# The scale, shift and gate vectors of a two-layer diffusion block: from 32-column matmuls to multiply-and-sum passes of VectorE

## The chip, the cores and the metric

The kernel runs on one core of a Trainium2 chip. The metric is the device time of one execution in microseconds: the median of three executions is 1672.93 us (1672.89 to 1675.74). About 0.2%, some 3.3 us, is what such a measurement can tell from no change.

## The reference

Two layers, each a token mixer and a mixture of experts, on 512 tokens (256 of context, 256 latent) of 1024 features. Ahead of each layer a conditioning vector gives six vectors of 1024: shift, scale and gate for the mixer and for the experts, for both conditions (context and latent).

```python
silu_c = jax.nn.silu(c)[:, None, :]
silu_cc = jax.nn.silu(c_ctx)
for l in range(DEPTH):
    sh1, sc1, g1, sh2, sc2, g2 = jnp.split(silu_c @ w_ada[l] + b_ada[l], 6, axis=-1)
    sh1c, sc1c, g1c, sh2c, sc2c, g2c = jnp.split(silu_cc @ w_ada[l] + b_ada[l], 6, axis=-1)
    hl = modulate(rmsnorm(xl, norm1[l]), sh1, sc1)
    hc = modulate(rmsnorm(xc, norm1[l]), sh1c, sc1c)
    yc, yl = token_mixer(hc, hl, ...)
    xl = xl + g1 * yl
    ...
```

`w_ada[l]` is 1024 x 6144 in float32, 24 MB a layer. The last layer needs of the context no more than shift and scale of the mixer.

## The kernel before

Features lie on the 128 partitions, tokens along the free axis. The program has four parts, one behind the other: the mixer of layer 0 (to about 640 us), the experts of layer 0 (to about 1040), the mixer of layer 1 (to about 1330) and the experts of layer 1.

**Products.** A weight matrix is used in units of two 128-row blocks, 512 KB each, which SyncE's queue loads into slots named `w` and `wa` (`Pipe.load_unit`, L161). Each unit is split into a high and a low part: ScalarE copies the high one (L102), VectorE subtracts (L103, 128x1024 elements). TensorE then makes three products for each block and chunk (`mm3`, L88 to L90) into four banks of PSUM. `Pipe` splits one unit ahead of the one in use.

**Modulation.** `ada` holds the six vectors as 48 chunks of 128 for each layer and both conditions. The first 2048 columns of layer 0 (shift and scale of the mixer, chunks 0 to 15) are made at the start from eight loads of 1 MB, in four steps that also give the normalised input `h`. All others come in half pieces of 512 columns (class `Ada`, L257): a half piece is 1 MB, loaded in two DMAs (`ada_load`, L252), and four matmuls (L283) whose stationary operand has 32 columns, of which two hold the silu of the conditions; the four write 32 rows each of one shared bank. Four pieces fill a bank; `finish` copies it (L294), sums and turns it by eight small matmuls (L297, records of both passes) and adds the bias (L304). A float32 matmul leaves two records in the profile.

**Where this work stands.** `tick` (L311) does one half piece behind each unit of weights that a product has used (`Pipe.matrix`, L204), from the gate projections of the mixer of layer 0 on. So 32 half pieces (layer 0's columns from 2048 on, layer 1's up to 4096) stand in the second half of that mixer. The last eight belong to the mixer of layer 1: five at its start (`TAIL`), while its norm is computed, and three in its first product.

**The order.** A scheduler lays out each engine's queue from the program, and may put an instruction ahead of others that stand before it in the code if its inputs and its buffer allow. Each engine then works strictly in that order. Around the change stand the norm and the first projections (`attention_proj`), the softmax tiles of the attention (`attention`: a score matmul L539, then on VectorE the maximum L541, its negative L543, after ScalarE's exponential L546 the reciprocal L548 and the scaling L549, then transposes on TensorE), the recurrence (`mlstm`), and three gated branches with two products per half (`branch`).

## Time and profile before

| | |
|---|---|
| median of three executions | 1672.93 us |
| span of the profiled execution | 1671.4 us |
| TensorE busy | 1582.0 us, 95% of the span |
| VectorE busy | 933.6 us, 56% |
| ScalarE busy | 712.6 us, 43% |
| GpSimd busy | 134.3 us, 8% |
| moved by DMA | 358.28 MB, mean 214 GB/s |

The profile gives the profiled execution's span from its first to its last instruction; the runs' own time lies around it, 1.5 us more at the median. Busy shares are averages over four parts with different limits, so what an edit is worth is read from the stretch in which it stands: in the mixer of layer 0 TensorE is busy nearly all the time and VectorE about half of it; in the experts of layer 0 both are close to full; in those of layer 1 the DMA queues are.

### The profile page before, as it was taken

What the parts mean: (1) busy time and instruction counts of PE and PEld (TensorE: products, weight loads), DVE (VectorE), ACT (ScalarE), POOL (GpSimd) and SP (SyncE); (2) the same over time, 40 slices, a digit from 0 to 9 for tenths busy, and PEclk for the clock granted to TensorE, in tenths of its full rate; (3) what the DMA queues carried; (4) which work ended last, traced back from release to release, by engine and by line L of the source; (5) the groups of instructions that cost most, each with busy time, mean ns of one, the idle gap of its engine ahead of it and who ended that gap; (6) DMA issues with size and microseconds to landing.
All of it is one profiled execution on the core that took longest, in us unless ns stands there. A gap on an engine that the chain in (4) does not pass through costs nothing. (4 is left out here: it accounts for less than half of the span.)

```text
span 1671.4 us, 22964 instructions
## 1 busy us (share of the span) xinstructions
PE 1582.0 (95%) x8611; PEld 1136.9 (68%) x8611; DVE 933.6 (56%) x1832; ACT 712.6 (43%) x1188; POOL 134.3 (8%) x128
## 2 busy tenths in 40 slices
PE   6999999999999999798989999999999998999998
PEld 3677767755567887577767776787689997453343
DVE  3565654723333443787877987567568666132223
ACT  2444336323232232476766786535466553110102
POOL 1000000000200011411211111010002001000000
PEclk8999999999999999799999999999999999999999
DMA  9222211476666375578998997623235776999996
GB/s 320 84 65 64 64 51 53 126 224 227 216 215 206 95 232 212 166 243 306 315 348 286 350 367 242 202 75 93 64 89 163 252 239 234 316 387 386 387 386 226
DMA packets 191210, 358.28 MB, mean 214 GB/s; under 512 B 13934, under 2 KB 30894, under 8 KB 190832
## 3 DMA queue, kind: packets, MB, share of 16 engines
q1 hardware_dynamic: 184160, 341.10, 60.4%
q0 software_dynamic: 6640, 15.53, 3.4%
q8 instruction: 70, 1.15, 0.3%
q14 instruction: 52, 0.43, 0.1%
q10 hardware_dynamic: 288, 0.07, 0.0%
HBM read 351.77 MB, written 12.60 MB: 218 GB/s over the span
## 5 line engine op out<-in xcount | busy, mean ns | idle before, releaser
L103 DVE TENSOR_TENSOR wlo<-wraw,whi 128x512 fp32r<-128x512 f32 (+4 forms) x356 | 322.2, 920 | 282.0 <-ACT whi L102 257.2
L102 ACT ACTIVATE whi<-wraw 128x512 fp32r<-128x512 f32 (+4 forms) x358 | 279.9, 802 | 356.0 <-PE mm L89 286.4
L88 PE MATMUL mm<-h,whi 128*128 128x512 f32 (+1 forms) x672 | 234.1, 354 | 4.1 <-ACT h L400 3.7
L89 PE MATMUL mm<-h,whi 128*128 128x512 f32 (+1 forms) x672 | 235.0, 353 | 0.0
L90 PE MATMUL mm<-h,wlo 128*128 128x512 f32 (+1 forms) x672 | 232.5, 351 | 1.3 <-DVE wlo L103 1.2
L88 PEld LDWEIGHTS mm<-h,whi 128*128 128x128 f32 x672 | 126.7, 190 | 35.8 <-issue 8.3
L89 PEld LDWEIGHTS mm<-h,whi 128*128 128x128 f32 x672 | 127.2, 190 | 30.9 <-issue 17.2
L90 PEld LDWEIGHTS mm<-h,wlo 128*128 128x128 f32 x672 | 126.9, 189 | 28.8 <-issue 12.1
L103 DVE TENSOR_TENSOR whl<-wraw,whl 128x1024 fp32r<-128x1024 f32 (+1 forms) x110 | 115.0, 1068 | 16.7 <-ACT whl L102 16.7
L1619 PE MATMUL mm<-wraw,x 128*64 128x512 f32 x504 | 121.2, 596 | 0.0
L102 ACT ACTIVATE whl<-wraw 128x1024 fp32r<-128x1024 f32 (+1 forms) x112 | 101.0, 931 | 19.9 <-issue 8.5
L283 PE MATMUL adps<-adw,sc 128*32 128x512 f32 (+1 forms) x448 | 80.3, 551 | 10.2 <-DMA adw<-in_w_ada 10.2
L1619 PEld LDWEIGHTS mm<-wraw,x 128*64 128x64 f32 x504 | 36.7, 137 | 67.5 <-issue 63.4
L88 PE MATMUL mm<-by,whi 128*128 128x512 f32 (+1 forms) x192 | 66.1, 344 | 0.0
L90 PE MATMUL mm<-whi,h 128*128 128x512 f32 x160 | 65.7, 413 | 0.0
L90 PE MATMUL mm<-by,wlo 128*128 128x512 f32 (+1 forms) x192 | 65.5, 341 | 0.0
L89 PE MATMUL mm<-by,whi 128*128 128x512 f32 (+1 forms) x192 | 65.2, 340 | 0.0
L88 PE MATMUL mm<-whi,h 128*128 128x512 f32 x160 | 65.0, 410 | 0.1
L89 PE MATMUL mm<-wlo,h 128*128 128x512 f32 x160 | 65.1, 407 | 0.0
L1570 PE MATMUL py<-wraw,gt 128*64 128x512 f32 x256 | 63.8, 598 | 0.7 <-ACT gt L1560 0.7
L88 PE MATMUL mm<-whi,x 128*128 128x512 f32 x128 | 53.6, 420 | 8.5 <-ACT whi L102 8.4
L546 ACT ACTIVATE pr<-sc,nm 128x512 f32<-128x512 f32 (+1 forms) x48 | 29.5, 615 | 62.6 <-DVE nm L543 59.6
(447 smaller groups left out, 2941.0 us busy)
## 6 DMA issues: line engine op xcount, KB each, us to landing
wraw<-in_e_w SPq DMA_DIRECT2D x278, 512.0 KB, 8.5
wraw<-in_w_in SPq DMA_DIRECT2D x96, 512.0 KB, 3.8
adw<-in_w_ada SPq DMA_DIRECT2D x80, 512.0 KB, 4.4
wraw<-in_e_w SPq DMA_DIRECT2D x33, 1024.0 KB, 13.4
wraw<-in_e_w SPq DMA_DIRECT2D x76, 256.0 KB, 6.1
adw<-in_w_ada SPq DMA_DIRECT2D x8, 1024.0 KB, 11.8
wraw<-in_w_out SPq DMA_DIRECT2D x16, 512.0 KB, 5.2
wraw<-in_w_pb SPq DMA_DIRECT2D x8, 512.0 KB, 4.8
```

The lines of the kernel that those rows point to most:

```text
L88: nc.tensor.matmul(ps, lh, rh, start=first, stop=False)
L89: nc.tensor.matmul(ps, lh, rl, start=False, stop=False)
L90: return nc.tensor.matmul(ps, ll, rh, start=False, stop=last)
L102: g.nc.scalar.activation(hi, src, AF.Copy)
L103: (eng or g.nc.vector).tensor_tensor(lo, src, hi.bitcast(F32), op=ALU.subtract)
L283: nc.tensor.matmul(self.ps[r:r + 32, :], g.sc62[:, k, 30 - 2 * j:62 - 2 * j], raw, start=(j == 0 and k < 4), stop=(j == n - 1 and k >= 4))
L546: last = nc.scalar.activation(pr[:, 0:w], sc[:, 0:w], AF.Exp, scale=ASC, bias=nm, accum_out=rs)
L1570: nc.tensor.matmul(py[hs, :], gt[:, k, hs], raws[s][:, kk, :], start=(k == 0), stop=(k == 3))
L1619: nc.tensor.matmul(ph[w][hs, :], x[:, k, hs], raws[s][:, kk, :], start=(k == 0), stop=(k == KT - 1))
```

## The change

The first four steps of layer 0 (chunks 0 to 15) stay as they were. All other chunks of both layers are no longer matmuls. The host passes their weights transposed (`w_adt`: one row of 1024 floats for each output feature). The silu of both conditions is spread once, at the start, over all partitions (`cbc`, two rows of 1024 on each partition: 16 small matmuls and four copies). For each chunk of 128 output features one load of 512 KB brings 128 rows, and VectorE makes one pass for each condition: multiply the rows by `cbc`, sum along the free axis from the bias on, write the sum into `ada`. Layer 0's chunks 16 to 47 and layer 1's 0 to 15 take two passes each, layer 1's 16 to 47 one pass (the latent condition; the other column is set to zero once): 48 chunks x 2 and 32 x 1, 128 passes in all. The transposed weights have two slots of their own (`ad`), and a step asks for the load of the next chunk. Ticks begin right behind the norm in both mixers. `w` and `wa` now alternate throughout. To make room, the descriptor space of GpSimd's own DMAs is cut to 2048 bytes a partition and `sc62` moves into a slot that is used again.

```diff
-LATER = 8
-TAIL = 5
-START1 = 8
-START0 = 18
-TAGS = dict(a=9, w=2, wa=2, wh=2, wl=2, h=8, t2=4, e1=2, e2=2, cz=2, b2=6)
+TAGS = dict(ad=2, a=9, w=2, wa=2, wh=2, wl=2, h=8, t2=4, e1=2, e2=2, cz=2, b2=6)
...
+class Rows:
+    def __init__(self, g, chunks):
+        self.g, self.chunks = g, list(chunks)
+        self.raws, self.k = [], 0
+
+    def left(self):
+        return len(self.chunks) - self.k
+
+    def load(self, n):
+        g = self.g
+        while len(self.raws) < min(n, len(self.chunks)):
+            l, j, _ = self.chunks[len(self.raws)]
+            raw = g.t([P, D], F32, "ad", "adw")
+            r = (j - 16 if l == 0 else 32 + j) * P
+            g.nc.sync.dma_start(raw, g.w_adt[r:r + P, :])
+            self.raws.append(raw)
+
+    def step(self):
+        g = self.g
+        self.load(self.k + 2)
+        l, j, conds = self.chunks[self.k]
+        raw = self.raws[self.k]
+        for s in conds:
+            out = raw if s == conds[-1] else g.t([P, D], BF16, "t2", "prod")
+            g.nc.vector.tensor_tensor_reduce(out=out, in0=raw, in1=g.cbc[:, s, :], scale=1.0,
+                                             scalar=g.vec[l][:, C_BADA + j:C_BADA + j + 1], op0=ALU.mult, op1=ALU.add,
+                                             accum_out=g.ada[l][:, j, s:s + 1])
+        self.raws[self.k] = None
+        self.k += 1
...
 def tick(g, n=1):
     for _ in range(n):
-        if g.pending:
-            b = g.pending[0]
-            b.step()
-            if not b.left():
-                g.pending.pop(0)
+        if g.rows.left():
+            g.rows.step()
...
 def mixer(g, l):
     if l == 0:
-        g.pipe = Pipe(g, lambda i: ("w", "wa")[i % 2] if i < START0 else "w", 1, ["w"])
+        g.pipe = Pipe(g, lambda i: ("w", "wa")[i % 2], 1, ["w"])
...
     else:
-        g.pipe = Pipe(g, lambda i: "w" if i < START1 else ("w", "wa")[i % 2], 1, ["w"])
+        g.pipe = Pipe(g, lambda i: ("w", "wa")[i % 2], 1, ["w"])
...
-        g.pipe.load(1)
+        g.pipe.load(2)
         g.pipe.single = True
-        b = g.pending[0]
-        raws = [b.load("h", i) for i in range(TAIL)]
-        for i in range(TAIL):
-            b.step(raws[i])
-        g.pipe.load(2)
...
-        g.ticking = True
+    g.ticking = True
     yb, gates, conv_q, last = attention_proj(g, l)
...
-    if l == 0:
-        g.ticking = True
     smo, gv, gu = gate_proj(g, l)
...
     if l:
+        tick(g, g.rows.left())
         g.router = router_prep(g, l)
...
     if l == 0:
-        tick(g, sum(b.left() for b in g.pending))
+        tick(g, g.rows.left())
...
-    g.sc62 = const("sc62", [P, KT, 62])
+    g.sc62 = g.t([P, KT, 62], F32, "b2", "sc62")
...
+    nc.gpsimd.memset(g.ada[1][:, 16:48, 0:1], 0.0)
...
-    g.pending = [Ada(g, l, range(a, b)) for l, a, b in ((0, 4, 8), (0, 8, 12), (1, 0, 4), (1, 4, LATER))]
+    g.cbc = const("cbc", [P, 2, D])
+    for s in range(2):
+        for q in range(2):
+            pc = g.bank([P, 512], "pcc")
+            for c in range(4):
+                nc.tensor.matmul(pc[:, c * P:(c + 1) * P], g.sc62[:, q * 4 + c, 30 + s:31 + s].to_broadcast([P, P]), g.ident, start=True, stop=True)
+            dst = g.cbc[:, s, q * 512:(q + 1) * 512]
+            if q:
+                nc.vector.tensor_copy(dst, pc)
+            else:
+                nc.scalar.activation(dst, pc, AF.Copy)
+    g.rows = Rows(g, [(0, j, (0, 1)) for j in range(16, 48)] + [(1, j, (0, 1)) for j in range(16)])
...
-    g.pending = [Ada(g, 1, range(LATER, 12))]
+    g.rows = Rows(g, [(1, j, (1,)) for j in range(16, 48)])
...
-    A['w_ada'] = f('w_ada')
+    A['w_ada'] = f('w_ada')[0:1, :, 0:2 * D]
+    wt = f('w_ada').transpose(0, 2, 1)
+    A['w_adt'] = np.concatenate([wt[0, 2 * D:], wt[1]], axis=0)
...
-    nc = _bacc.Bacc("TRN2", target_bir_lowering=False, num_devices=1)
+    nc = _bacc.Bacc("TRN2", target_bir_lowering=False, num_devices=1, dynamic_dma_scratch_size=2048)
```

How the change moves instructions is shown at three places. Line numbers of the changed kernel differ: its L99 is the subtraction L103 of before, its L84 to L86 are the products L88 to L90, its L333 is the new pass.

TensorE, in the gate projections and first branch of the mixer of layer 0 (`adps` is the shared bank of the modulation, `adw` its weights; each row of two is half of a half piece). Before:

```order
L88 MATMUL mm<-h,whi 128x512
L89 MATMUL mm<-h,whi 128x512
L283 MATMUL adps<-adw,sc_71 32x512 x2
L90 MATMUL mm<-h,wlo 128x512
L88 MATMUL mm<-h,whi 128x512
```

Now, at the change from the first branch product to the second (`by` is the attention's output, split):

```order
L86 MATMUL mm<-h,wlo 128x512
L84 MATMUL mm<-by,whi 128x512
L85 MATMUL mm<-by,whi 128x512
L86 MATMUL mm<-by,wlo 128x512
L84 MATMUL mm<-by,whi 128x512
```

The products stand next to each other; from the first score matmul of layer 0 on, no matmul of the modulation is left in the program.

VectorE, in the fourth softmax tile of the attention of layer 0 (`mx` maximum, `nm` its negative, `arc` reciprocal, `pr` probabilities, `pts` transposed probabilities, `va` values). Before:

```order
L541 TENSOR_REDUCE mx<-sc 128x1
L478 TENSOR_TENSOR rt<-mm,rope 128x256
L543 TENSOR_SCALAR nm<-mx 128x1
L479 TENSOR_TENSOR rt<-mm,rope 128x256
L103 TENSOR_TENSOR wlo<-wraw,whi 128x1024
L548 RECIPROCAL arc<-ars 128x1
L549 TENSOR_SCALAR pr<-pr,arc 128x256
L555 COPY pts<-pt 128x256
```

Now (each pass is a row `L333 ISA` of 128x1024 and, behind it, the read-out of its sum; a chunk's first pass writes its products to `prod`, its second over the weights):

```order
L567 TENSOR_REDUCE mx<-sc 128x1
L333 ISA prod,ada_132<-adw,cbc,vec_78 128x1024
L333 ISA ada_132 128x1
L569 TENSOR_SCALAR nm<-mx 128x1
L333 ISA prod,ada_132<-adw,cbc,vec_78 128x1024
L333 ISA ada_132 128x1
L574 RECIPROCAL arc<-ars 128x1
L333 ISA adw,ada_132<-adw,cbc,vec_78 128x1024
L333 ISA ada_132 128x1
L575 TENSOR_SCALAR pr<-pr,arc 128x256
L333 ISA adw,ada_132<-adw,cbc,vec_78 128x1024
L333 ISA ada_132 128x1
```

Passes now stand between the steps of a softmax. Of the 128 passes 28 stand ahead of the first maximum of layer 0's attention, 40 between the first and the seventeenth of its 32, 4 behind that, and 56 behind the recurrence, those of layer 1's chunks 16 to 47 among them: the scheduler has put all of these ahead, into the mixer of layer 0, and the mixer of layer 1 has none.

VectorE, at the third step of the modulation that stays (the bias is added, then `A` is the scale, `u` and `h` the normalised input). Before:

```order
L304 TENSOR_TENSOR ada_132<-adpo,vec_78 128x4 x2
L374 SCALAR_TENSOR_TENSOR A<-ada_132,vec_78 128x4
L399 SCALAR_TENSOR_TENSOR u<-xT,A,rr 128x256 x3
L401 SCALAR_TENSOR_TENSOR h<-u,ada_132,h 128x256
```

Now:

```order
L99 TENSOR_TENSOR wlo<-wraw,whi 128x1024 x2
L333 ISA prod,ada_132<-adw,cbc,vec_78 128x1024
L333 ISA ada_132 128x1
L300 TENSOR_TENSOR ada_132<-adpo,vec_78 128x4
L333 ISA adw,ada_132<-adw,cbc,vec_78 128x1024
L333 ISA ada_132 128x1
L300 TENSOR_TENSOR ada_132<-adpo,vec_78 128x4
L400 SCALAR_TENSOR_TENSOR A<-ada_132,vec_78 128x4
L425 SCALAR_TENSOR_TENSOR u<-xT,A,rr 128x256 x3
```

The first passes stand ahead of the third part of `h`.

In SyncE's queue the loads of the transposed weights now stand one or two at a time between those of the mixer of layer 0, from behind its fourth unit to its last branch; the sixteen half-megabyte loads at the start of the mixer of layer 1 are gone. On TensorE 320 products of 128x512 stand between the first and the seventeenth score matmul of layer 0, where there were 177.

## Rows read from the trace of the kernel before

**Rows 1.** The page: span, and busy time, share and instructions of two engines.

```profile
span 1671.4 us, 22964 instructions
...
PE 1582.0 (95%) x8611; PEld 1136.9 (68%) x8611; DVE 933.6 (56%) x1832; ACT 712.6 (43%) x1188; POOL 134.3 (8%) x128
```

**Rows 2.** Table by stretches of the mixer of layer 0, from start to end.

```profile
core 0: us, PE busy (x) PEld busy (x) DVE busy (x) ACT busy (x) POOL busy (x), PEclk, DMA share, GB/s
25.00:126.00 101.00, 95.76 (x512) 69.95 (x513) 56.85 (x128) 39.56 (x70) 4.05 (x2) 0.95 0.38 119
126.00:201.00 75.00, 74.37 (x390) 53.48 (x389) 46.07 (x114) 32.76 (x68) 0.00 (x0) 1.00 0.22 64
201.00:275.00 74.00, 73.81 (x385) 52.53 (x384) 35.11 (x84) 34.47 (x71) 0.00 (x0) 1.00 0.18 50
320.00:425.00 105.00, 99.81 (x413) 53.82 (x412) 33.72 (x50) 30.15 (x33) 3.14 (x4) 1.00 0.70 225
425.00:640.00 215.00, 214.01 (x985) 153.48 (x983) 82.51 (x119) 59.98 (x87) 19.82 (x28) 1.00 0.63 203
```

**Rows 3.** The same table, of the modulation's matmuls (`adps`) alone.

```profile
core 0: us, PE busy (x) PEld busy (x) ACT busy (x), PEclk, DMA share, GB/s
320.00:560.00 240.00, 59.02 (x256) 8.17 (x256) 2.40 (x4) 1.00 0.65 209
1056.00:1075.00 19.00, 3.17 (x16) 0.45 (x16) 0.60 (x1) 1.00 0.75 228
```

**Rows 4.** Timeline of TensorE around half of a half piece.

```profile
start us, us, engine line op out<-in xcount [idle before <-releaser]
341.50 0.39 PE L90 MATMUL mm<-h,wlo 128*128 128x512 f32 x1
341.73 0.39 PE L88 MATMUL mm<-h,whi 128*128 128x512 f32 x1
342.05 1.05 PE L283 MATMUL adps<-adw,sc 128*32 128x512 f32 x4
343.03 0.50 PE L89 MATMUL mm<-h,whi 128*128 128x512 f32 x1
```

**Rows 5.** Timeline of TensorE at the turning of a full bank.

```profile
371.78 0.39 PE L90 MATMUL mm<-h,wlo 128*128 128x512 f32 x1
372.01 0.95 PE L297 MATMUL adpo<-lsel,ev 128*128 128x8 f32 x8
372.82 0.48 PE L88 MATMUL mm<-h,whi 128*128 128x512 f32 x1
```

**Rows 6.** Waits for the modulation's weights, 320 to 560: total us, times, longest.

```profile
PE adps L283 <- DMA adw<-in_w_ada: 5.5, 6, 2.3
```

**Rows 7.** The same, start of the mixer of layer 1 (1053 to 1075).

```profile
PE adps L283 <- DMA adw<-in_w_ada: 0.9, 1, 0.9
```

**Rows 8.** Timeline of TensorE and VectorE at the norm of layer 1.

```profile
1045.53 2.96 PE L283 MATMUL adps<-adw,sc 128*32 128x512 f32 x20
...
1046.03 0.69 DVE L345 COPY sp<-ss 128x512 f32<-128x512 f32 x1 [1.89 <-PE ss L337]
...
1046.74 0.06 DVE L615 MEMSET mp<- 8x5 f32 x1
...
1048.42 1.05 PE L347 MATMUL sst<-lsel,sp 128*128 128x1 f32 x8
```

**Rows 9.** Groups of VectorE by shape: busy us, mean ns, idle before.

```profile
L103 DVE TENSOR_TENSOR wlo<-wraw,whi 128x1024 fp32r<-128x1024 f32 x150 | 182.8, 1221 | 210.5 <-ACT whi L102 187.2 <-PE mm L90 22.3 <-DMA wraw<-in_e_w 0.3
...
L399 DVE SCALAR_TENSOR_TENSOR u<-xT,A,rr 128x256 f32<-128x256 f32 x22 | 9.6, 476 | 1.7 <-PE rr L364 1.6
L401 DVE SCALAR_TENSOR_TENSOR h<-u,ada,h 128x256 fp32r<-128x256 f32 x22 | 9.6, 479 | 0.1
...
L849 DVE SCALAR_TENSOR_TENSOR yg<-pg,vec,gbs 128x128 f32<-128x128 f32 x24 | 6.7, 339 | 4.1 <-PE pg L845 4.1
...
L617 DVE TENSOR_TENSOR_SCAN Mr<-ar,mp 8x128 f32<-8x128 f32 x8 | 3.8, 469 | 0.1
```

**Rows 10.** Group of ScalarE: the read-out of a sum.

```profile
L546 ACT ACTIVATION_READ_ACCUMULATOR pr<-sc,nm 128x1 f32 x48 | 9.3, 194 | 0.0
```

**Rows 11.** Timeline of VectorE: first and seventeenth maximum of layer 0's attention.

```profile
127.86 0.41 DVE L541 TENSOR_REDUCE mx<-sc 128x1 f32<-128x256 f32 x1
...
200.95 0.42 DVE L541 TENSOR_REDUCE mx<-sc 128x1 f32<-128x256 f32 x1
```

**Rows 12.** Two shorter stretches, columns as in Rows 2.

```profile
100.00:125.00 25.00, 21.79 (x95) 16.98 (x93) 19.19 (x52) 11.61 (x21) 4.05 (x2) 0.86 0.22 71
300.00:325.00 25.00, 24.62 (x182) 21.05 (x182) 22.18 (x58) 11.35 (x23) 2.49 (x2) 1.00 0.41 127
```

**Rows 13.** Timeline of TensorE: two waits, at 19 and at 116 us.

```profile
19.45 1.93 PE L283 MATMUL adps<-adw,sc 128*32 128x256 f32 x16 [3.72 <-DMA adw<-in_w_ada]
...
115.97 0.96 PE L90 MATMUL mm<-nhl,wlo 128*128 128x512 f32 x3 [2.66 <-DVE wlo L103]
```

**Rows 14.** The page: loads of the modulation's weights, KB each, us to landing.

```profile
adw<-in_w_ada SPq DMA_DIRECT2D x80, 512.0 KB, 4.4
```

More of the change, by code (lines that the diff above doesn't have):

```diff
@@ L1706, in block_kernel @@
     g.nc, g.tc = nc, tc
-    g.w_ada, g.w_in, g.w_gk, g.w_uq2, g.a_wukv = w_ada, w_in, w_gk, w_uq2, a_wukv
+    g.w_ada, g.w_adt, g.w_in, g.w_gk, g.w_uq2, g.a_wukv = w_ada, w_adt, w_in, w_gk, w_uq2, a_wukv
     g.x_t = x_t
```

2 lines of the change are left out of this document (1 added, 1 removed).

## The prediction, made before the changed kernel ran

> **What bounds the kernel now.** I read the busy times of the page first: TensorE is busy for 1582 of 1671.4 us, VectorE for 934 [rows 1]. An average over four parts says little, so the table by stretches comes next, for the mixer of layer 0, where nearly all of the removed work stands. The reader should compare two columns there: TensorE is busy for 94 to 100% of every stretch, VectorE for 56.9 of 101 us ahead of the attention, 46.1 of 75 in its first half, 35.1 of 74 in its second, and for less than 40% from 320 us on [rows 2]. So TensorE bounds the mixer, and what leaves its queue there shortens the mixer by as much, if nothing else gets in its way. Where it does wait, the waits view and the timeline say for what: between 320 and 560 for the modulation's own weights [rows 6].
>
> **What is removed in the mixer of layer 0.** Its modulation matmuls fill 59.0 us of TensorE between 320 and 560 [rows 3]. That these are on TensorE's path and not beside other matmuls shows in the timeline: products follow each other every 0.23 us (341.50, 341.73), and around one group of modulation matmuls the next product starts 1.30 us behind the last, 1.07 more than the pace, which is the group's own 1.05 [rows 4]. Four banks are turned by small matmuls; there the next product starts 1.04 us behind the last, 0.81 more than the pace [rows 5], 4 x 0.81 = 3.2. And TensorE stands still for 5.5 us until these weights have landed [rows 6]. Together 59.0 + 3.2 + 5.5 = **67.7 us**.
>
> **What is removed in the mixer of layer 1.** Its first product holds 3.2 us of such matmuls [rows 3], one turning of 0.8 and one wait of 0.9 [rows 7], 4.9 in all. Ahead of it five half pieces stand beside the norm. That chain is short of work for TensorE, so most of them cost nothing; but twenty records fill TensorE from 1045.53 on, and the small norm matmul, whose input VectorE has ready at 1046.72, starts at 1048.42 [rows 8]: 1.7 us. Together 4.9 + 1.7 = **6.6 us**. The mixer of layer 1 gets no passes in return, by the order.
>
> So 67.7 + 6.6 = **74.3 us** of TensorE's path go.
>
> **What a pass costs.** The trace has no multiply-and-sum. The nearest row is the subtraction of two 128x1024 operands in SBUF, 1.22 us [rows 9]; reading out the sum is bounded by VectorE's shortest instruction, 0.06 [rows 8], and ScalarE's read-out of a sum, 0.19 [rows 10]. I take 1.22 + 0.15 = 1.37 us. From above I bound the pass by the one row in which VectorE carries a value from element to element, the scan: over 128 elements it takes 469 ns where a plain operation of this width takes 339 [rows 9], 130 ns / 128 = 1.0 ns an element more. For 1024 elements that is 1.22 + 1.04 + 0.15 = 2.4 us. I take the lower value, because a sum needs no scan and the subtraction has the same operands; the upper one is kept as a rival. 128 passes x 1.37 = 175 us of VectorE, against 74 taken from TensorE: the change pays only where VectorE was idle.
>
> **Where the passes lie.** By the order all 128 stand in the mixer of layer 0.
> - Ahead of the attention, 25 to 126 us: 28 x 1.37 = 38.4 on top of 56.9 [rows 2], 95 of 101 us.
> - First sixteen softmax tiles, 127.9 to 201.0, 73 us [rows 11]. Here 40 passes, 54.8 us, join 46.1 [rows 2]; the scheduler has also moved 320 - 177 = 143 products here, which brings 143 x 0.23 = 33 us for TensorE and six subtractions, 7 us, for VectorE. VectorE then has 108 us of work, TensorE 73 + 33 = 106.
> - Second half of the attention: 4 passes, hidden in a stretch half idle.
> - Behind the recurrence: 56 passes, 77 us, on top of 33.7 + 82.5 = 116 [rows 2], 193 in all. TensorE keeps 320 us, less 67.7, less the 33 that moved forward: 219. They fit, beside the products, which use weights split one unit ahead.
>
> So the passes are covered by TensorE's products, but in the first two stretches the cover is used up, and what is late next is a softmax step or a split on which TensorE waits. From below this costs about 1.5%: at 300 to 325 us VectorE was busy for 22.2 of 25 us and TensorE still for 24.6 [rows 12]. Over 101 + 106 us that is 3. [...] I take **17 us**, nearer to the lower row since the scheduler has put enough products between the softmax steps: 8 ahead of the attention, where the first passes stand in front of the third part of the input and wait for a load; 2 for the two us by which VectorE has more work than TensorE in the softmax tiles; 5 for sixteen softmax steps that each find a pass in front of them for 0.6 us on average, half of it covered; 2 for the clock.
>
> **What costs nothing, and why.** Spreading the silu puts 16 small matmuls and four copies of some 0.7 us (the copy of that size) [rows 8] ahead of the norm; the first modulation step waits for its weights until 19.45, 3.7 us [rows 13], and covers the two copies of VectorE in its path. SyncE's queue gets 80 loads of 512 KB, 40 MB, in the mixer of layer 0 in place of 32, and 8 MB fewer in layer 1; the queues are at 0.20 to 0.38 of their time to 275 us, where most of the moved loads go [rows 2]. A chunk of two passes, 2.7 us, needs a load that lands in 4.4 [rows 14]; with one more chunk in its second slot and 3 us of other VectorE work per chunk, it is in time, unless the queue is held up (a rival). If that cover is gone, each chunk costs up to 4.4 - 2.7 = 1.7 us.
>
> **The sum.** The page gives the span, 1671.4 us; the median of the runs, 1672.9, lies 1.5 above it, and I count that as what lies around the span. 1672.9 - 67.7 - 6.6 + 17 = 1615.6, say **1616 us**. The ends of the unknown cost give 1602 and 1655.
>
> [...] Two rows bear on operands in SBUF: the operation on `h` and `u`, both in SBUF, takes 479 ns, the one with `rr` in PSUM 476 [rows 9]; a second float32 operand in SBUF costs nothing there, but neither row keeps a sum. [...]
>
> **Rivals.**
> 1. *Slower: passes at the scan's pace.* Place: VectorE ahead of the attention and in its first half. At 2.4 us a pass VectorE has 56.9 + 67 = 124 us of work ahead of the attention where TensorE has 101, 53 + 96 = 149 in the sixteen tiles against 106, and 116 + 134 = 250 behind the recurrence, less 8 that moved, against 219: 23 + 43 + 23 = 89 us too much, and 10 more for the softmax steps. 1672.9 - 74.3 + 99 = **1698**. The loss begins where these excesses reach 74: at about 2.2 us a pass. For it: the scan's row; against it: the subtraction's and the two rows without a penalty. Chance 0.09.
> 2. *Faster, but less: passes wait for their loads.* VectorE works in order, so a pass whose rows haven't landed holds every split behind it. 34 chunks up to the seventeenth tile x 1.7 us is 58 at worst; two fifths of it on top of the forecast, 24, gives **1640**. For it: two slots only, and a queue shared with the weights; against: the free DMA time [rows 2]. Chance 0.14.
> 3. *No change.* If something other than TensorE paced the second half of the mixer, the time would stay at **1672**. Against it: 99.8 of 105 and 214 of 215 us busy, and DMA at 0.63 to 0.70 [rows 2]. Chance 0.03.
>
> **How the numbers follow.** The forecast has 0.74. The range runs from 1595, a cost of 3 us and 7 for what the sum may have missed (loads and buffers of the modulation that no longer hold up others), to 1655, the upper bound of the stall; the second rival lies in it, the first and third don't. Faster by over 0.2% (3.3 us, what a measurement can tell): 0.74 + 0.14, less 0.01 for a second rival at its worst: 0.87. Same: 0.03 and that 0.01: 0.04. Slower: 0.09.
>
> **What would show it right or wrong.** Right: no modulation matmul behind 60 us; passes of 1.2 to 1.4 us; the recurrence of layer 0 ends at about the same time as before or somewhat later (more products are behind it by then), the mixer of layer 0 some 50 us earlier, that of layer 1 about 6 us shorter; VectorE busy above 90% between 25 and 230 us and TensorE idle for about 15 us there. Wrong: passes of 2 us or more; waits of VectorE for the transposed weights of more than 20 us; TensorE waiting for VectorE in the branches behind the recurrence; or experts of layer 0 that start late because their first loads now come behind the modulation's.

## The result, and the profile after

The changed kernel takes **1634.62 us** (median of four runs, 1633.29 to 1636.02) against 1674.01 for the kernel before on the same chip: ratio 0.9759, 95% interval 0.9739 to 0.9778. It is faster by 39.4 us; the forecast was 57. The time lies in the range that was given, and the sign is right; 18 us of the expected gain are missing. The experiments look for these.

The page of the changed kernel, its span and the busy time of each engine:

```profile
span 1631.5 us, 22596 instructions
PE 1519.4 (93%) x8283; PEld 1137.8 (70%) x8283; DVE 1083.0 (66%) x2085; ACT 710.5 (44%) x1185; POOL 129.7 (8%) x129
```

Against [rows 1], TensorE has some 63 us less, VectorE 149 more. The passes and their read-out, with what VectorE waited for ahead of them (columns: ns of one, shortest/median/longest; first and last start in us):

```profile
L333 DVE DVE_READ_ACCUMULATOR2_ANT ada<- x128: 70/83/89, 47.3 to 555.6; 128x1 f32 x128
L333 DVE CUSTOM_DVE_ANT_0 adw<-adw,cbc,vec x80: 1178/1280/1291, 47.4 to 554.4; 128x1024 f32<-128x1024 f32 x80
L333 DVE CUSTOM_DVE_ANT_0 prod<-adw,cbc,vec x48: 1265/1278/2772, 46.1 to 445.2; 128x1024 bf16<-128x1024 f32 x48
...
its engine sat idle before it (us, times) until:
  DMA adw<-in_w_adt: 29.6, 27
```

A pass is 1.28 + 0.08 = 1.36 us; the forecast took 1.37. All 128 lie between 46 and 556 us, in the mixer of layer 0, as the order had it.

Three marks show where the time went: the first maximum of the attention (`mx`), the first ST of the recurrence, the first output of the mixer. In each row the first start that is named (the time behind the three durations) belongs to layer 0. Of the kernel before:

```profile
L541 DVE TENSOR_REDUCE mx<-sc x48: 411/690/692, 127.9 to 1216.6; 128x1 f32<-128x512 f32 x32, 128x1 f32<-128x256 f32 x16
L745 ACT ACTIVATE ST<-pst x6: 597/598/647, 276.3 to 1243.8; 128x512 f32<-128x512 f32 x6
L1049 DVE SCALAR_TENSOR_TENSOR xT<-mm,ada,xT x24: 472/474/485, 641.7 to 1397.3; 128x256 f32<-128x256 f32 x24
```

Of the changed kernel:

```profile
L567 DVE TENSOR_REDUCE mx<-sc x48: 414/688/692, 148.1 to 1176.4; 128x1 f32<-128x512 f32 x32, 128x1 f32<-128x256 f32 x16
L771 ACT ACTIVATE ST<-pst x6: 597/597/599, 332.6 to 1203.6; 128x512 f32<-128x512 f32 x6
L1069 DVE SCALAR_TENSOR_TENSOR xT<-mm,ada,xT x24: 474/477/485, 608.0 to 1356.1; 128x256 f32<-128x256 f32 x24
```

- **Ahead of the attention** it lost 148.1 - 127.9 = 20.2 us.
- **From there to the first ST** 184.5 us in place of 148.4, 36.1 more. By the order 158 more products stand ahead of the first `pst` (850 against 692), and at the pace of [rows 4], 0.23, they take 36.3. So the softmax tiles lost nothing. The seventeenth maximum, for [rows 11], in the timeline of VectorE, with a pass right behind it:

```profile
254.37 0.42 DVE L567 TENSOR_REDUCE mx<-sc 128x1 f32<-128x256 f32 x1
254.82 1.29 DVE L333 CUSTOM_DVE_ANT_0 prod<-adw,cbc,vec 128x1024 bf16<-128x1024 f32 x1
```

- **From the first ST to the first output** 275.4 us in place of 365.4. Without 67.7 us of modulation and the 36.3 of products that moved, it should be 261.4: 14.0 us lost. It is rather 17: behind the first output 118 products of 128x512 are left where 104 were (counted in the traces, to the last output), and 14 x 0.23 = 3.2 us of work have thus left this stretch too.

The sum, 20.2 - 0.2 + 14.0 = **34 us of stall**, stands where the prediction had 17. The mixer of layer 0 comes out 33.7 us earlier (641.7 to 608.0), which is 67.7 - 34. Its last output, with the 14 products behind it as well, comes 33.0 us earlier (667.05 to 634.09), so the stall is 34 to 35 us by either mark.

The table by stretches shows both places (columns as in [rows 2]: busy time of PE, PEld, DVE, ACT, POOL; granted clock; DMA share; GB/s):

```profile
25.00:50.00 25.00, 20.53 (x136) 13.03 (x134) 11.92 (x27) 6.55 (x12) 0.00 (x0) 0.84 0.96 310
50.00:75.00 25.00, 23.60 (x97) 19.13 (x98) 22.42 (x44) 9.78 (x19) 0.00 (x0) 0.92 0.50 169
75.00:100.00 25.00, 24.55 (x114) 16.69 (x113) 15.78 (x25) 7.65 (x13) 0.00 (x0) 1.00 0.41 141
100.00:125.00 25.00, 17.55 (x89) 14.23 (x89) 20.61 (x54) 7.13 (x12) 0.00 (x0) 0.81 0.29 92
125.00:150.00 25.00, 20.60 (x86) 16.54 (x85) 21.36 (x43) 9.52 (x19) 4.72 (x2) 0.78 0.32 106
375.00:400.00 25.00, 14.18 (x64) 10.93 (x63) 19.88 (x37) 15.78 (x17) 14.07 (x20) 0.91 0.29 88
400.00:425.00 25.00, 19.71 (x92) 15.23 (x91) 23.92 (x49) 2.12 (x2) 0.00 (x0) 0.95 0.48 165
```

TensorE, 21.79 of 25 us at 100 to 125 before [rows 12], has 17.55, and its clock falls on average to 0.81. Three things can be read from the trace as the cause, and each became a theory.

1. **The start.** ScalarE has two splits of weights ahead of the third modulation step's copy (`ev`) and waits for their loads; TensorE waits for `ev` (4.3 us, the 45.21 row below). Timelines of ScalarE and TensorE:

```profile
36.38 1.06 ACT L98 ACTIVATE whi<-wraw 128x1024 fp32r<-128x1024 f32 x1 [2.57 <-DMA wraw<-in_w_gk]
43.83 1.06 ACT L98 ACTIVATE whi<-wraw 128x1024 fp32r<-128x1024 f32 x1 [6.39 <-DMA wraw<-in_w_gk]
44.80 0.37 ACT L290 ACTIVATE ev<-adps 128x256 f32<-128x256 f32 x1
...
45.21 1.01 PE L293 MATMUL adpo<-lsel,ev 128*128 128x4 f32 x4 [4.27 <-ACT ev L290]
```

2. **The gate chain.** The recurrence's gates are some twenty small operations that go to and fro between VectorE and TensorE, from `gS` to `nM` (lines 604 to 676). Passes stand between them; in the waits of TensorE, 90 to 130, one row has nearly all (columns: us in total, times, longest):

```profile
PE mm L84 <- DVE mp L644: 6.7, 1, 6.7
```

The granted clock falls in this wait, from 1.00 at 118.5 to 0.50 from 119.5 us on. Between 121 and 128.5 TensorE is busy all the time at 0.50, and products follow each other every 0.43 us, where [rows 4] has 0.23 (rows of TensorE's timeline, then of the table by stretches):

```profile
120.68 0.77 PE L84 MATMUL mm<-nhl,whi 128*128 128x512 f32 x1 [6.73 <-DVE mp L644]
127.61 0.63 PE L84 MATMUL mm<-nhl,whi 128*128 128x512 f32 x1
128.03 0.63 PE L85 MATMUL mm<-nhl,whi 128*128 128x512 f32 x1
...
121.00:128.50 7.50, 7.50 (x24) 5.95 (x24) 5.44 (x25) 0.31 (x1) 0.00 (x0) 0.50 0.14 51
```

3. **GpSimd behind the recurrence.** The scheduler now has twelve of the router's diagonal matrices ahead of the last two squares. VectorE waits for these, ScalarE's square root for VectorE, the next split for the square root, TensorE for the split (8.6 us). One row of each engine's timeline, in the order of the chain:

```profile
376.66 8.37 POOL L1122 TENSOR_SCALAR diag<-ident,A 128x128 f32<-128x128 f32 x12 [11.96 <-DVE dn L800]
...
386.07 0.69 DVE L842 TENSOR_REDUCE ms<-sqg 128x4 f32<-128x512 f32 x1 [4.41 <-POOL sqg L841]
...
392.90 0.32 ACT L860 ACTIVATE ms<-ms,eps 128x32 f32<-128x32 f32 x1 [6.52 <-DVE ms L842]
...
399.05 0.80 PE L86 MATMUL mm<-by,wlo 128*128 128x512 f32 x1 [8.59 <-DVE wlo L99]
```

### The profile page after: what moved, and what is told of

The parts are those of the page before. It is cut to its first block, busy times and chain, and to the rows that moved or that the text cites. A ratio compares the mean times of both kernels' runs of the same rounds, so it can differ in the third digit from the quotient of the medians.

```text
span 1631.5 us, 22596 instructions
## 1 busy us (share of the span) xinstructions
PE 1519.4 (93%) x8283; PEld 1137.8 (70%) x8283; DVE 1083.0 (66%) x2085; ACT 710.5 (44%) x1185; POOL 129.7 (8%) x129
## 5 line engine op out<-in xcount | busy, mean ns | idle before, releaser
L99 DVE TENSOR_TENSOR wlo<-wraw,whi 128x512 fp32r<-128x512 f32 (+4 forms) x356 | 321.4, 917 | 130.9 <-ACT whi L98 127.6
L84 PE MATMUL mm<-h,whi 128*128 128x512 f32 (+1 forms) x672 | 236.8, 359 | 9.6 <-DVE bt L934 3.3
L85 PE MATMUL mm<-h,whi 128*128 128x512 f32 (+1 forms) x672 | 237.5, 354 | 0.0
L86 PE MATMUL mm<-h,wlo 128*128 128x512 f32 (+1 forms) x672 | 234.2, 354 | 1.3 <-DVE wlo L99 1.1
L84 PEld LDWEIGHTS mm<-h,whi 128*128 128x128 f32 x672 | 129.2, 194 | 34.6 <-DVE bt L934 6.0
L86 PEld LDWEIGHTS mm<-h,wlo 128*128 128x128 f32 x672 | 128.9, 193 | 20.4 <-issue 3.0
L85 PEld LDWEIGHTS mm<-h,whi 128*128 128x128 f32 x672 | 129.9, 193 | 18.6 <-issue 4.3
L99 DVE TENSOR_TENSOR whl<-wraw,whl 128x1024 fp32r<-128x1024 f32 (+1 forms) x110 | 115.1, 1069 | 15.2 <-ACT whl L98 15.2
L1639 PE MATMUL mm<-wraw,x 128*64 128x512 f32 x504 | 121.2, 596 | 0.0
L333 DVE CUSTOM_DVE_ANT_0 adw<-adw,cbc,vec 128x1024 f32<-128x1024 f32 x80 | 101.9, 1279 | 24.5 <-DMA adw<-in_w_adt 24.5
L86 PE MATMUL mm<-by,wlo 128*128 128x512 f32 (+1 forms) x192 | 65.4, 343 | 8.6 <-DVE wlo L99 8.6
L84 PE MATMUL mm<-by,whi 128*128 128x512 f32 (+1 forms) x192 | 66.0, 344 | 2.2 <-ACT sg L920 2.2
L333 DVE CUSTOM_DVE_ANT_0 prod<-adw,cbc,vec 128x1024 bf16<-128x1024 f32 x48 | 62.6, 1309 | 5.2 <-DMA adw<-in_w_adt 5.1
L84 PE MATMUL mm<-whi,h 128*128 128x512 f32 x160 | 65.4, 413 | 0.1
L86 PE MATMUL mm<-whi,h 128*128 128x512 f32 x160 | 64.8, 405 | 0.0
L84 PE MATMUL mm<-whi,x 128*128 128x512 f32 x128 | 53.6, 420 | 8.7 <-ACT whi L98 8.6
```

The costliest lines, as they stand in the source:

```text
L84: nc.tensor.matmul(ps, lh, rh, start=first, stop=False)
L85: nc.tensor.matmul(ps, lh, rl, start=False, stop=False)
L86: return nc.tensor.matmul(ps, ll, rh, start=False, stop=last)
L99: (eng or g.nc.vector).tensor_tensor(lo, src, hi.bitcast(F32), op=ALU.subtract)
L333: g.nc.vector.tensor_tensor_reduce(out=out, in0=raw, in1=g.cbc[:, s, :], scale=1.0, scalar=g.vec[l][:, C_BADA + j:C_BADA + j + 1], op0=ALU ...
L1639: nc.tensor.matmul(ph[w][hs, :], x[:, k, hs], raws[s][:, kk, :], start=(k == 0), stop=(k == KT - 1))
```

## The experiments

`issue_after` in the diffs queues an instruction behind a named one of the same engine. No pass is left out, except in the last two runs. All marks of the runs, from one profile of each, in us (outputs: from the start of the first output of the mixer to that of the last; experts: from there to the first output of the experts of layer 0, called their end here; mixer 1: from there to the first output of the mixer of layer 1). The order of VectorE, ScalarE and GpSimd ahead of the first maximum is the same in the changed kernel and in the run on GpSimd's order, and yet that mark differs by 2.2 us; a single difference of two microseconds therefore shows little. Each group of four runs was timed beside the kernel before, which took 1677.2, 1676.4 and 1674.7 us there; so ratios are compared.

| run | first maximum | to first ST | to first output | outputs | experts | mixer 1 | us | ratio, 95% interval |
|---|---|---|---|---|---|---|---|---|
| before | 127.9 | 148.4 | 365.4 | 25.4 | 363.7 | 354.3 | | 1 |
| changed | 148.1 | 184.5 | 275.4 | 26.1 | 361.0 | 348.8 | 1634.6 | 0.9759 (0.9739 to 0.9778) |
| GpSimd order | 145.9 | 184.0 | 273.8 | 26.1 | 363.6 | 348.3 | 1631.1 | 0.9721 (0.9703 to 0.9739) |
| start | 138.3 | 184.4 | 270.4 | 26.1 | 368.2 | 365.7 | 1639.4 | 0.9760 (0.9740 to 0.9780) |
| gates | 137.4 | 184.9 | 271.7 | 26.1 | 363.4 | 370.4 | 1643.6 | 0.9793 (0.9777 to 0.9810) |
| all three | 137.4 | 185.6 | 270.2 | 26.1 | 365.2 | 367.3 | 1638.8 | 0.9762 (0.9745 to 0.9778) |
| clean start | 137.3 | 183.6 | 276.2 | 26.1 | 363.8 | 348.8 | 1627.9 | 0.9717 (0.9683 to 0.9751) |
| late passes | 147.6 | 177.1 | 270.5 | 31.8 | 367.9 | 348.6 | 1632.3 | 0.9739 (0.9706 to 0.9772) |
| quiet chain | 124.9 | 180.8 | 272.2 | 28.7 | 365.4 | 348.8 | 1610.6 | 0.9617 (0.9583 to 0.9652) |
| quiet, late, GpSimd | 124.6 | 180.9 | 267.4 | 33.9 | 365.3 | 348.4 | 1608.9 | 0.9603 (0.9569 to 0.9636) |
| quiet, GpSimd | 125.3 | 180.8 | 270.8 | 29.3 | 363.0 | 348.9 | **1606.1** | **0.9580** (0.9560 to 0.9600) |
| none before the maximum | 121.2 | 182.9 | 269.5 | 33.7 | 370.0 | 348.8 | 1615.6 | 0.9637 (0.9617 to 0.9657) |

### GpSimd's order

```diff
-            nc.gpsimd.tensor_scalar(diag[k, s], g.ident, A[:, k, s:s + 1], None, op0=ALU.mult)
+            with g.tc.issue_after(g.sqh.ins):
+                nc.gpsimd.tensor_scalar(diag[k, s], g.ident, A[:, k, s:s + 1], None, op0=ALU.mult)
```

(`g.sqh` is the last `sqg` of the recurrence.)

> The changed kernel, with one edit: the router's diagonal matrices are issued on GpSimd only after the squares of the recurrence's output, as before. The passes stay where they are. Theory (some 10 us are lost where GpSimd has twelve of the router's operations ahead of the last two squares, which holds VectorE, then ScalarE's square root, then the next split and TensorE): TensorE's wait of 8.6 us at 399 goes, and most of its slow clock there, the mixer of layer 0 ends 8 to 13 us earlier, time 1622 to 1627. Rival (VectorE is simply full there, and the wait only moves to the next split): under 4 us gained, 1631 to 1635.

The ratio is 0.9721; its interval touches the changed kernel's at 0.9739. But where the theory had its loss the run hardly gains: from the first ST to the first output 273.8 us, 1.6 fewer, and the mixer ends 4.3 us earlier, not 8 to 13; 2.2 of these lie ahead of the attention, where the order is the same in both runs, and can't be put down to the edit. The rival's forecast, 1631 to 1635, has the time. The waits of TensorE at 370 to 420 show that the wait behind `diag` did shrink, from 8.6 to 3.5:

```profile
PE mm L86 <- DVE wlo L99: 3.5, 1, 3.5
PE pg L871 <- DVE gp L868: 3.3, 2, 2.5
PE mm L84 <- ACT sg L920: 2.2, 1, 2.2
```

What was saved was lost again further on. The third theory was right about the chain of waits and wrong about its price.

### The start

```diff
-            if self.g.ticking:
+            if self.g.ticking and not self.g.first:
                 tick(self.g)
...
-            nc.vector.scalar_tensor_tensor(g.h[k][:, 1, a:b], u[:, a:b], B(k, s), g.h[k][:, 0, a:b].bitcast(F32),
+            g.hold = nc.vector.scalar_tensor_tensor(g.h[k][:, 1, a:b], u[:, a:b], B(k, s), g.h[k][:, 0, a:b].bitcast(F32),
...
-            g.nc.vector.tensor_tensor_reduce(out=out, in0=raw, in1=g.cbc[:, s, :], scale=1.0,
+            with g.tc.issue_after(g.hold.ins):
+                g.nc.vector.tensor_tensor_reduce(out=out, in0=raw, in1=g.cbc[:, s, :], scale=1.0,
```

> The changed kernel, with one edit: no pass and no load of transposed weights is asked for until the four parts of the mixer's input are all under way; so passes start four later, and the scheduler puts as many at the other end. Theory (at the start ScalarE waits for weights of which the landing was late, ahead of the third modulation step, and passes stand ahead of the input's third part): TensorE's wait of 4.3 us at 41 goes and the first maximum of the attention comes 4 to 8 us earlier, at 140 to 144; time 1627 to 1631. Rival (VectorE's total work ahead of the attention sets the time there, wherever it stands): the first maximum stays within 2 us of 148, time 1633 to 1636.

ScalarE's order is right again: `ev` runs at 37.90, and the first maximum comes at 138.3, 9.8 us earlier and better than the 140 to 144 expected. The time is the same, though. The table says why: the mixer of layer 1 takes 365.7 us in place of 348.8. `g.hold` was set by the norm of layer 1 too, and so the 32 passes of layer 1's second set, which the scheduler had put into the mixer of layer 0, came to stand in the mixer of layer 1, at 16.9 / 32 = 0.5 us each. The side effect tells something of its own: 1.36 us of a pass cost 0.5 there, and 0.7 in the next run, the gates', where that mixer takes 370.4 us.

### The gate chain, and all three

```diff
-    nc.vector.tensor_copy(nM, pR[0:96])
+    g.hold = nc.vector.tensor_copy(nM, pR[0:96])
```

> The edit of the run before, and no pass is issued between the start of the recurrence's gate chain and its end (eight passes move behind it, none is left out). Theory (the chain of small operations between VectorE and TensorE is stretched by the passes between its steps, while TensorE has nothing else): the copy that ends the chain comes at 112 to 118 in place of 130, TensorE's waits there (6.7 and 4.2 us) go, its clock stays over 0.95 of full speed, and the first maximum comes at 130 to 136; time 1616 to 1623. Rival (as many passes as before ahead of the attention, so the same time): the first maximum stays at 140 or later, time within 3 us of the run before.

> All three edits together. Theory (three separate losses, that add): the gain of the gates' run and that of GpSimd's run in sum, 1606 to 1616, which takes in the time that the prediction gave. Rival (what is gained ahead of the attention is lost again behind the recurrence, where VectorE then has less time for the passes): no more than 4 us better than the better one of the two.

Both have the same side effect in layer 1, so their times can't test what was expected of them, and only their columns of layer 0 are read. The chain ends at 114.0, where it ended at 120.7 in the run on the start and at 130.4 in the changed kernel (timelines of VectorE), and the waits for `mp` and `qT` are gone; yet the first maximum comes at 137.4, 0.9 us earlier than in the run on the start. The twelve passes now stand between the chain's end and the maximum, and TensorE waits there (waits of TensorE, 100 to 140):

```profile
PE mm L86 <- DVE nm L570: 6.6, 1, 6.6
PE mm L84 <- DVE va L539: 2.9, 1, 2.9
```

By the trace 18 more products stand ahead of the first maximum than in the run on the start (305 and 287), 4.1 us at 0.23, so that mark hides part of a gain; but by the first output of the mixer nothing of it is left (594.0 against 593.1). So the rival held: not the place of the passes between the steps counts, but that they stand in that stretch at all. The second theory fell in this form.

### The clean start

The run on the start, with `g.hold` set in layer 0 only.

> The edit of the second run, without its side effect: there the layer-1 passes had come to stand behind the input of the mixer of layer 1, and that mixer took 17 us longer; here they stay in the mixer of layer 0. Theory (the second run gained 10 us ahead of the attention and lost it again in layer 1): the first maximum at 137 to 140, the mixer of layer 1 as long as with the changed kernel (from its first output back to the experts' end 348 to 350 us), time 1622 to 1628. Rival (VectorE is full behind the recurrence, so that four passes more there give the gain back): output of the mixer of layer 0 from 604 us on, time 1630 or more.

Mixer 1 is back at 348.8, the first maximum at 137.3. The theory held: the ratio is 0.9717, some 7 us better than the changed kernel, though the intervals overlap at their ends, and 1627.9 us lies at the edge of the 1622 to 1628 expected. The mixer of layer 0 comes out at 597.2, 10.8 us earlier than in the changed kernel, all of it gained ahead of the attention. Beside the run on the start it tells what passes cost behind the recurrence: 32 more stand there, and from the first ST to the first output it takes 276.2 us in place of 270.4, 0.18 each.

### The passes of layer 1 late

```diff
-        if g.rows.left():
+        if g.rows.left() and (g.gated or g.rows.chunks[g.rows.k][0] == 0):
...
+            g.gated = nc.vector.tensor_tensor(yc[:, :, ts_], y, gu[:, :, ts_], op=ALU.mult)
+        if l == 0:
+            g.hold = g.gated
```

> The changed kernel, with one edit: the passes of layer 1, which nobody needs before 1000 us, are issued only after the gated part of the mixer of layer 0 (the last yc). The order of GpSimd stays as in the changed kernel. Theory (behind the recurrence, 375 to 450 us, VectorE is over 90% busy with passes and its other work, and TensorE waits for whatever is behind them; GpSimd's order is only the last link): from the recurrence's first ST to the first output 260 to 269 us in place of 275, time 1620 to 1628. Rival (GpSimd's diagonal matrices are what holds TensorE there, passes or not): 272 us or more, time 1631 or more.

A new theory, and a gain that was given back. None of the passes stands between the first ST and the last `yc` (13 did), that part takes 81.7 us in place of 91.5, and the first output comes 12.8 us earlier (595.2). From the first ST to the first output it is 270.5, more than the 260 to 269 expected, and the time, 1632.3, is the rival's (1631 or more) and not the 1620 to 1628 of the theory. But now seven passes stand between the mixer's outputs on VectorE, and their loads are late (timeline of VectorE):

```profile
600.69 0.68 DVE L364 TENSOR_TENSOR sq<-xT 128x512 f32<-128x512 f32 x1
608.67 1.28 DVE L336 CUSTOM_DVE_ANT_0 adw<-adw,cbc,vec 128x1024 f32<-128x1024 f32 x1 [7.29 <-DMA adw<-in_w_adt]
609.88 0.08 DVE L336 DVE_READ_ACCUMULATOR2_ANT ada<- 128x1 f32 x1
609.88 1.22 DVE L99 TENSOR_TENSOR wlo<-wraw,whi 128x1024 fp32r<-128x1024 f32 x1
```

VectorE stands still for 7.3 us ahead of a pass that nobody needs before layer 1, with a split behind it that TensorE needs. The outputs take 31.8 us in place of 26.1, the experts 367.9 in place of 361.0. That is the second rival of the prediction, passes that wait for their loads, in a place where it had not been looked for.

### The quiet chain

```diff
              lambda c, ps: nc.scalar.activation(akr[:, c, :], ps, AF.Copy))
+    g.ticking = l == 1
...
-            nc.vector.tensor_scalar(nm, mx, -ASC, None, op0=ALU.mult)
+            nmi = nc.vector.tensor_scalar(nm, mx, -ASC, None, op0=ALU.mult)
+            if not g.ticking:
+                g.ticking, g.hold = True, nmi
```

> The edit of the run on the clean start, and no pass between the start of the gate chain and the first maximum of the attention: twelve move behind it, none is left out. Theory (in that stretch it is the number of passes that costs, not their place between the steps, since the gates' run had the chain 7 us shorter and the first maximum only 1 us earlier): the first maximum at 128 to 132, against 127.9 before the change; if the twelve cost nothing where they go, time 1614 to 1620. Rival (the passes ahead of the chain set it): the first maximum at 135 or later. The passes that come later find VectorE full behind the recurrence: 2 to 6 us may be lost there.

The clean start, with no pass from `gS` to the first maximum: 1610.6 us, ratio 0.9617. The first maximum comes at 124.9, 12.4 us earlier than in the run on the clean start and earlier than before the change. The table by stretches:

```profile
25.00:50.00 25.00, 24.97 (x165) 16.96 (x163) 12.53 (x34) 9.19 (x18) 0.00 (x0) 0.95 0.90 293
50.00:75.00 25.00, 23.82 (x99) 17.34 (x99) 23.55 (x38) 10.10 (x16) 0.00 (x0) 1.00 0.70 222
75.00:100.00 25.00, 25.00 (x128) 19.13 (x127) 13.75 (x25) 10.09 (x17) 0.00 (x0) 1.00 0.22 68
100.00:125.00 25.00, 22.69 (x128) 17.25 (x127) 18.61 (x60) 11.00 (x20) 3.73 (x2) 1.00 0.22 67
125.00:150.00 25.00, 24.05 (x122) 18.28 (x121) 22.85 (x48) 13.96 (x28) 0.00 (x0) 1.00 0.58 177
```

That is better than the theory had it (128 to 132, and 1614 at best). At 50 to 75 VectorE is as full as anywhere (23.55 of 25) and TensorE still has 23.82: next to products passes cost little. At 100 to 125, where the changed kernel had TensorE at 17.55 us and its clock at 0.81, it now has 22.69 and 1.00. The twelve passes took 12 x 1.36 = 16.3 us of VectorE in the chain and cost 12.4 there, 1.03 each, at the first maximum. At the mixer's first output the gain is 19.4 us (597.2 to 577.8), more than these twelve passes last; what gained the other 7 us behind the first maximum, no run tells.

Part of it is lost again in the outputs: five passes now stand between them, VectorE waits for their loads, once for 7.2 us, and the last eight outputs follow each other only from 603.82 on (timeline of VectorE):

```profile
591.27 1.29 DVE L334 CUSTOM_DVE_ANT_0 adw<-adw,cbc,vec 128x1024 f32<-128x1024 f32 x1 [7.21 <-DMA adw<-in_w_adt]
603.82 3.22 DVE L1075 SCALAR_TENSOR_TENSOR xT<-mm,ada,xT 128x256 f32<-128x256 f32 x8
```

The outputs take 28.7 us in place of the 26.1 of the clean start, within the 2 to 6 us that were expected to be lost.

### Quiet chain, late passes and GpSimd's order

> The clean start, the quiet chain, the late layer-1 passes and the order of GpSimd, all together; no pass is left out. Theory (the stall of 34 us was lost in the stretch from the gates to the first maximum and in the one behind the recurrence, in both because passes joined an already busy VectorE): first maximum at 128 to 132, from the first ST to the first output 258 to 268 us, time 1598 to 1612. Rival (the passes cost TensorE's time wherever they stand): 1618 or more.

1608.9, within the forecast of the theory, with the first output at 572.9 and a larger loss in the outputs, 33.9 us, seven passes between them. Beside the quiet chain's run the interval tells no difference.

### Quiet chain and GpSimd's order

> The quiet chain with GpSimd's order, the layer-1 passes left free to stand where the scheduler puts them. Theory (behind the recurrence VectorE is full for some 75 us whatever stands in GpSimd's queue, so a shorter queue only moves the wait): within 4 us of the quiet chain's run, 1607 to 1612, the last yc 5 to 8 us earlier but the first output of the mixer under 4 us earlier. Rival (the queue is the loss, as the first run supposed): 8 us or more, 1603 or less.

1606.1, the lowest of all and just under the 1607 to 1612 expected: 0.9580, 1.8% under the changed kernel by the ratios (0.9580 / 0.9759 = 0.982). Against the quiet chain alone the spans differ by 2.4 us (1605.9 and 1608.3), and the intervals overlap. From the first ST to the first output it is 1.4 us less, but of this 0.4 is left at the last output (606.2 and 606.6); the rest of the difference lies in the experts. The last `yc` comes 2.3 us earlier (393.6 and 395.9), not 5 to 8. So GpSimd's order is worth 1 to 2 us in its stretch, as in the first run (1.6) and between the gates' run and that on all three (271.7 and 270.2), and hardly anything at the mixer's end.

### None before the maximum

The twelve passes that stood ahead of the gates also held back (`g.ticking = l == 1` ahead of `attention_proj` in place of the edit of the start).

> The quiet chain, and none of the passes ahead of the attention at all: the twelve that stood ahead of the gate chain also move behind the first maximum; none is left out. Theory (ahead of the gates TensorE has products for every step, so that passes cost nothing there, and the loss was in the chain alone): the first maximum at 122 to 125, no more than 3 us earlier than in the quiet chain's run, and the time the same or up to 6 us longer, since twelve more passes stand where VectorE is full: 1609 to 1617. Rival (every pass ahead of the attention costs, 0.5 us or more of each): first maximum at 119 or earlier, time 1603 to 1608.

The first maximum comes 3.7 us earlier, a little more than expected. Eight products fewer stand ahead of it (284 and 292, in the traces), 1.8 us, so that the twelve passes themselves cost 1.9, under 0.2 us each. The end is 5 us later than in the quiet chain's run by span (1613.6): fourteen passes come to stand behind the first output, seven of them between the outputs, which take 33.7 us in place of 28.7; the last output is then 0.7 us later (607.3), and the other 4.6 us lie in the experts. The ratios, 0.9637 and 0.9617, have overlapping intervals.

### Without layer 1's passes, and without their loads

```diff
-        for s in conds:
+        for s in conds if l == 0 else ():
...
-    g.rows = Rows(g, [(0, j, (0, 1)) for j in range(16, 48)] + [(1, j, (0, 1)) for j in range(16)])
+    g.rows = Rows(g, [(0, j, (0, 1)) for j in range(16, 48)])
```

The first line is the first run, both the second; on the quiet chain. Layer 1's modulation is zero in both; one execution of each took 5330.5 and 5327.4 us, nearly all of the excess in the experts of layer 1. Only the mixer of layer 0 is read: in the first of the two runs the granted clock averages 0.98 from 306 to 570 us, against 0.97 in the quiet chain's run from 306 to 578.

> The quiet chain with the 64 passes of layer 1 left out (the modulation of layer 1 is zero, so only the mixer of layer 0 is read); their loads are still made. That takes 87 us from VectorE behind the recurrence. Theory (VectorE, full from the recurrence's end on, holds TensorE there): from the first ST to the first output 255 to 264 us in place of 272. Rival (TensorE's own work sets that stretch and its waits there come from the chain of the gated part): 268 us or more.

> The run before, with the loads of those passes left out as well, 24 MB less to move in the mixer of layer 0. Theory (VectorE's time, not the loads, is what the passes cost): within 2 us of the run before from the first ST to the first output. Rival (the loads of the transposed weights hold up the weights of the products): 3 us or more less; the experts of layer 0 may start with more of their weights loaded, and be a few us shorter.

Marks of the first of the two:

```profile
L777 ACT ACTIVATE ST<-pst x6: 592/597/597, 306.4 to 1171.3; 128x512 f32<-128x512 f32 x6
L1075 DVE SCALAR_TENSOR_TENSOR xT<-mm,ada,xT x24: 474/478/484, 570.0 to 1324.4; 128x256 f32<-128x256 f32 x24
```

and of the second:

```profile
L777 ACT ACTIVATE ST<-pst x6: 592/597/597, 306.1 to 1168.0; 128x512 f32<-128x512 f32 x6
L1075 DVE SCALAR_TENSOR_TENSOR xT<-mm,ada,xT x24: 473/478/484, 569.8 to 1321.1; 128x256 f32<-128x256 f32 x24
```

263.6 us without the passes, against 272.2 with them; 263.7 without the loads too. Of the 64 passes 59 stood in that stretch, 80 us of VectorE; they cost 8.6 us of it, 0.15 each on average, and their loads nothing. The other five stood between the outputs, which now take 26.1 us in place of 28.7. The theory held at its upper end.

The average hides where the cost lies. The last `yc`, the end of the gated part, stands in the timelines of the quiet chain's run and of that without the passes at

```profile
395.87 0.69 DVE L882 TENSOR_TENSOR yc<-yg,gu 128x512 f32<-128x512 f32 x1
390.09 0.69 DVE L882 TENSOR_TENSOR yc<-yg,gu 128x512 f32<-128x512 f32 x1
```

so from the first ST to it 90.2 us have become 83.7, and from it to the first output 182.0 have become 179.9. Five passes ahead of the last `yc` cost 6.5 us, 54 behind it 2.1; counted with the five products that stand on the other side of that mark, 5.4 and 3.2. The pair of runs that differs by the late passes alone says the same: with eight passes there in place of thirteen, 87.4 us have become 80.8. So a pass costs about 1 us in the gated part too, and little beside the products behind it: 0.04 to 0.06 us here, and 0.18 by the 32 passes of the clean start, which all stand behind the last `yc`.

## Why the prediction was right, and where it was short

**The terms of the removal held.** By the marks the mixer of layer 0 is 33.7 us shorter, which is the 67.7 us forecast less the 34 of stall, a stall that was itself worked out with the 67.7. What bears on the 67.7 by itself is the run without layer 1's passes: there 153 products more than before stand ahead of the first ST (by the order) and 14 more behind the first output, 38.4 us in all, and 365.4 - 67.7 - 38.4 = 259.3 us stand against 263.6 measured. So at least 63.4 us went; whether the other 4.3 are the stall of the eight passes that are left there, or were never to be had, is not shown. From the experts' end to the first output of layer 1 it is 348.8 in place of 354.3, 5.5 us less; the forecast was 6.6.

**The pass held:** 1.36 us measured, 1.37 forecast. That excludes the first rival, passes at the pace of a scan. The sum costs next to nothing: the subtraction of two operands of the same size, both in SBUF as well, takes 1.22 [rows 9], the pass 1.28. Its read-out takes another 0.08.

**The step that failed is the stall, 17 us.** Its size was half of what came, and it lay elsewhere than the text put it. That the time still lies in the range is in part luck: the stall had been sought in the first two stretches alone, and 14 to 17 of the 34 us fell in the third, for which the text had nothing. The range's upper end, 1655, allows a stall of 56 us (1655 - 1672.9 + 74.3), the author's estimate; no run shows it, and by the marks the stall was 34 to 35. Term by term:

- *"8 ahead of the attention"*: 20.2. Undone step by step, 10.8 us belong to the start (passes, their loads and ScalarE's order there), 12.4 to twelve passes between the gates and the first maximum, 3.7 to the twelve ahead of the gates (1.9 of it theirs); that is 27 in sum, more than 20, since without any pass the first maximum comes earlier than before the change, at 121.2. Of these 6.7 us, 4.1 are there at the third `ev` already (41.3 before, 37.2 then); why, was not tested. The prediction had compared 95 us of work with 101 us of time, a mean over the whole stretch. The row of 100 to 125 us was the place itself: VectorE had 19.19 of 25 us there and TensorE, with 21.79, idled already [rows 12]. Sixteen microseconds of passes do not fit into 5.8.
- The 2 for the softmax tiles' excess of VectorE and *"5 for sixteen softmax steps"*: nothing. From the first to the seventeenth maximum it is 254.4 - 148.1 = 106.3 us, which is just the 106 of TensorE's work; the scheduler had given each step enough products, and a VectorE that was busy for 95.7 of these 106 us, less than the 108 worked out, held up nobody.
- *"They fit"*, behind the recurrence: 14.0, or 17 with the products that moved behind the first output. The text had counted 193 us of work against 219, again a mean. VectorE has 23.92 of 25 us at 400 to 425, where the gated part of the mixer goes to and fro between the engines. On the quiet chain the passes of layer 1 are 8.6 us of it, most of them the few in the gated part, and GpSimd's order 1.4 to 1.6; the rest, 4 to 7 us, is not told apart.
- *"2 for the clock"* was an estimate that no run shows; the runs showed 3 us or more. The granted clock averaged 0.81 and 0.78 between 100 and 150, where [rows 12] has 0.86 from 100 to 125, and is 1.00 in the quiet chain's run. In the changed kernel 16 products follow each other there every 0.43 us in place of 0.23, which is 3.2 us (an estimate from the timeline), part of the 12.4.

**The signs that were named.** VectorE waited 29.6 us for transposed weights, over the 20 that were to speak for the second rival. By the trace 25.4 of these lie between the last `yc` and the first output, where the passes cost TensorE 2 to 6 us in all by two pairs of runs, and only 3.4 ahead of the seventeenth maximum, where the rival had put its loss. So that sign was badly chosen: idle time of VectorE cost something where a needed split stood behind it, as between the outputs in the late passes' run (a wait of 7.3 us; 31.8 us in place of 26.1). "TensorE waiting for VectorE in the branches behind the recurrence" was rightly named as a sign against. Between 25 and 230 us VectorE was to be busy above 90% and TensorE idle for about 15 us; VectorE was busy for 164.1 of 205 us, 80%, and TensorE idle for 19.4. So it was not a full VectorE that held TensorE up there, but passes in the way of a few operations that TensorE waited for.

**What stays open.** The experts of layer 0 take between 361.0 and 370.0 us in the runs that keep all passes, also where no pass stands near them; no run was made for that. What the quiet chain gained behind the first maximum has no explanation either. More than two slots for the transposed weights were not tried.

## What to carry to other kernels

Work that moved to an engine with idle time was nearly free here only where that idle time lay beside another engine's independent work; find the chains that go to and fro between two engines, and keep the moved work out of them: passes of 1.36 us cost about 1 us each in the two chains of this mixer (twelve in the gate chain, five in the gated part), under 0.2 ahead of the first, nothing that shows in the softmax tiles, and 0.04 to 0.18 beside the products at the end. Compare busy time by stretches as short as those chains, not by means over a hundred microseconds. And work that was moved late, because nobody needed it yet, still held up the queue in which it stood when its load was late: VectorE stood still for 7.3 us ahead of one pass in the late passes' run.

## What the runs showed of the hardware

- A multiply-and-sum pass over 128x1024 float32 with both operands in SBUF takes 1.28 us on VectorE, the read-out of the sum 0.08, whether the products are written as float32 or as bf16 (medians of 1.280 and 1.278).
- Between 100 and 150 us TensorE's granted clock averaged 0.81 and 0.78 in the changed kernel, where TensorE was busy for 17.55 and 20.60 of 25 us, and 1.00 in the quiet chain's run, where it was busy for 22.69 and 24.05. Behind a wait of 6.7 us it was 0.50 from 121 to 128.5 us, and products followed each other every 0.43 us in place of 0.23.
